# Gated DeltaNet in a hybrid encoder block: decayed keys per chunk in full 128-row tiles, one buffer of U, the queries' norms later

## The chip, the core and the metric

The kernel runs on one core of a Trainium2 chip. The metric is the device time of one execution in microseconds (us). Three runs of the kernel before gave 1604.98, 1605.38 and 1606.62 us; the median is 1605.38 us.

The core's engines are TensorE (PE: matmuls, with its weight loads listed apart as PEld), VectorE (DVE), ScalarE (ACT), GpSimd (POOL) and SyncE (SP), which issues the DMAs here. Each engine works through its own instructions in the order in which they were written into the program, and waits on semaphores for the others.

## The reference

One layer on a sequence of 1024 positions with 1024 channels: an RMS norm, one projection to all branches, a gated DeltaNet (4 heads, key and value width 128), a banded attention (8 heads), two gates, an output projection, and a feed-forward part with a short convolution. The change is in the DeltaNet. It works in chunks of 64 positions; per head a state S (128 x 128) goes from chunk to chunk:

```python
def step(s, xs):
    w_i, uv_i, p_i, qg_i, kd_i, gl_i = xs
    u = uv_i - jnp.einsum('bhid,bhde->bhie', w_i, s)
    o = jnp.einsum('bhid,bhde->bhie', qg_i, s) + jnp.einsum('bhij,bhje->bhie', p_i, u)
    s = gl_i[..., None, None] * s + jnp.einsum('bhid,bhie->bhde', kd_i, u)
    return s, o
```

`w` and `uv` come from a triangular solve in each chunk, `kd` are the keys of the chunk times their decay to its end: `kd_c = k * jnp.exp(G[..., -1:] - G)[..., None]`. The einsum with `kd` sums over the 64 positions of one chunk.

## The kernel before

Two chunks stand together on the 128 partitions as a pair p (8 pairs, `NT`); e is the chunk in the pair and `r` its 64 partitions. The big projections (`proj_half`, lines 118 to 133) are matmuls of 128 x 128 weights with 512 columns into `psph`, three for each product (high and low halves of both operands). For each of the four heads h these steps follow one another:

- `gdn_qkv`: three projections and convolutions (`conv_silu`) give keys `kf`, values `vf` and queries in `WQ`.
- `gdn_prep`: PE transposes the keys into PSUM (`psk`), ACT copies them to `nKs`, writes the decayed keys `Kd` (line 431) and squares them (`jk`, line 433) into the sums `ssk`. From `ssk` POOL computes the norm's factors up to `nks`.
- `gdn_prep2`: PE transposes the values (`psv`), ACT copies them to `Vs`; decay matrices (`psd`, `decb`, `decT`), the products of the keys (`psG`, `psQ`), the matrix `nL`, which goes through DRAM to `Lr`. These, `psW`, `psU` and `psk` all take tiles of one PSUM pool, `psa`, which has three buffers: a fourth tile waits until the first is read.
- `gdn_solve`: 31 pairs of DVE instructions (`tmp`, `Zt`, lines 506 and 508) invert the 32 x 32 blocks; the result goes through DRAM to `zt`.
- `gdn_apply`: PE finishes the inverse (`psB`, `psZ`) and makes W (`psW`) and U (`psU`).
- `gdn_chain`: the 16 steps of the state. Per step PE multiplies with S (`psws`, line 568), DVE updates the 64 rows of U (line 569) and writes O (line 570), PE multiplies `Kd` with U (`pss`, line 572), DVE makes the next S (line 574). After the second chunk of a pair comes `pso` (line 578).
- `gdn_rms`, `gdn_out`, `gdn_qnorm`: norm and output of O; `gdn_qnorm` squares the queries into `sqq`, and PE sums them (`psn`).

The loop over heads (lines 652 to 716) interleaves the chain of head h with the preparation of head h + 1. The tuples C1, C2, C3, OUT, APP, APK and QN say after how many steps each part is placed, and a scheduler with priorities (`tc.high_priority`, `behind()`) then sets the order on each engine; the projections of the coming head and of the gates fill PE in between. At the start `first_rms` (line 224) loads x in blocks of 128 rows (`xt`) into tiles that are free by then, and `wv` (line 268) are the first values' weights.

Of the kernel before, what the change touches and what calls it, by code (L numbers as in the profile page):

```python
# [8 lines left out]
F32 = mybir.dt.float32  # L9
F32R = mybir.dt.float32r  # L10
# [6 lines left out]
P = 128  # L17
D = 1024
# [16 lines left out]
OUT = (0, 3, 5, 3, 8)  # L35
APP = (10, 10, 10, 2)
APK = (7, 4, 3, None)
QN = (7, 3, 4, 5)
PR0 = 1
GFILL = (4, 4, 5, 5, 4)  # L40
PRI = 4000
# [5 lines left out]
def hybrid_kernel(ctx: ExitStack, tc: tile.TileContext, a):  # L47
# [176 lines left out]
    def first_rms(e):  # L224

        s = slice(e * HN, (e + 1) * HN)
        psr = psa.tile([P, HN], F32, tag="a", name="psrb")
        for i in range(4):
            xt = gp.tile([P, D], F32, tag=("Kd", "U")[i % 2], name="xt", bufs=2)
            nc.sync.dma_start(xt, a["x"][(4 * e + i) * P:(4 * e + i + 1) * P, :])  # L230
            ssq = sml.tile([P, 1], F32, tag="ssq", name="ssq")
            nc.scalar.activation(xt, xt, AF.Square, accum_out=ssq)
            ms = sml.tile([P, 1], F32, tag="ms", name="ms")
            nc.vector.tensor_scalar(out=ms, in0=ssq, scalar1=1.0 / D, scalar2=EPS, op0=ALU.mult, op1=ALU.add)
            rs = sml.tile([P, 1], F32, tag="rs", name="rs")
            rsqrt(rs, ms)
            dg = gp.tile([P, P], F32, tag=("Zt", "tmp", "Z11", "B1")[i], name="dg")
            nc.vector.tensor_scalar_mul(dg, ident, rs)
            mm(psr[:, i * P:(i + 1) * P], ones2, dg, start=True, stop=True)
        nc.scalar.copy(rb[:, s], psr)  # L240
# [24 lines left out]
    nea = prm[:, 61:65]  # L265
    nc.scalar.activation(nea, nea, AF.Exp)
    nc.vector.tensor_scalar_mul(nea, nea, -1.0)
    wraw, whi, wlo = (gw.tile([P, KT, P], dt, tag=tg, name="wv") for dt, tg in ((F32, "sq"), (F32R, "nKs"), (F32R, "Vs")))
    nc.sync.dma_start(wraw, a["w_tiles"][2 * GH])
    split(wraw, whi, wlo, nc.vector)  # L270
    ws.append((whi, wlo))
# [82 lines left out]
    for i in range(1):  # L354
        t_ = gp.tile([P, NT, P], F32, name=f"zt{i}")
        nc.gpsimd.memset(t_, 0.0)
        zts.append(t_)

    def bc3(ap, n):

        return ap.unsqueeze(2).broadcast_to([P, NT, n])
# [38 lines left out]
    def gdn_prep(c):  # L400
        h, WQ, kf, vf = c["h"], c["WQ"], c["kf"], c["vf"]
        qv = WQ[:, :, 64:192]

        m64 = [m_.unsqueeze(1).broadcast_to([P, NT, CH]) for m_ in (mgt64, mle64)]
        gms = []
        for m_, n_ in zip(m64, ("gs", "gi")):
            gh = gp.tile([P, NT, CH], F32R, tag="gmh", name=n_ + "h")
            gl = gp.tile([P, NT, CH], F32R, tag="gml", name=n_ + "l")
            en = nc.gpsimd if n_ == "gs" else nc.vector
            en.tensor_tensor(out=gh, in0=m_, in1=bc3(ghi.bitcast(F32)[:, :, h], CH), op=ALU.mult)  # L410
            en.tensor_tensor(out=gl, in0=m_, in1=bc3(glo.bitcast(F32)[:, :, h], CH), op=ALU.mult)
            gms.append((gh.rearrange("p n j -> p (n j)"), gl.rearrange("p n j -> p (n j)")))
        nKs = gw.tile([P, NT, P], F32, tag="nKs", name="nKs")
        Kd = gp.tile([P, NT, P], F32, tag="Kd", name="Kd", bufs=2)
        Vs = gw.tile([P, NT, P], F32, tag="Vs", name="Vs")
        ssk = gp.tile([P, NT], F32, tag="ssk", name="ssk", bufs=2)
        rk = gp.tile([P, NT], F32, tag="rk", name="rk", bufs=2)
        bv = gp.tile([P, NT], F32, tag="bv", name="bv", bufs=2)
        nb = gp.tile([P, NT], F32, tag="nb", name="nb", bufs=2)
        nks = gp.tile([P, NT], F32, tag="nks", name="nks", bufs=2)  # L420
        jk = gp.tile([P, P], F32, tag="jk", name="jk")
        pks = []
        for e in range(2):
            psk = psa.tile([P, HN], F32, tag="a", name="psk")
            for i in range(4):
                p = 4 * e + i
                nc.tensor.transpose(out=psk[:, i * P:(i + 1) * P], in_=kf[:, p * P:(p + 1) * P], identity=ident)
            pks.append(psk.rearrange("p (n d) -> p n d", d=P))
            nc.scalar.copy(nKs[:, 4 * e:4 * e + 4, :], pks[e])
            for i in range(4):  # L430
                nc.scalar.activation(Kd[:, 4 * e + i, :], pks[e][:, i, :], AF.Copy, scale=eg[:, 2, 4 * e + i, h:h + 1])
            for i in range(4):
                nc.scalar.activation(jk, nKs[:, 4 * e + i, :], AF.Square, accum_out=ssk[:, 4 * e + i:4 * e + i + 1])
        nc.vector.tensor_scalar_add(ssk, ssk, EPS)
        rsqrt(rk, ssk)
        nc.gpsimd.tensor_mul(bv, beta[:, :, h], rk)
        nc.gpsimd.tensor_mul(nb, bv, rk)
        nc.gpsimd.tensor_mul(nks, nb, neg0[:, :, h])
        c.update(nKs=nKs, Kd=Kd, Vs=Vs, nks=nks, bv=bv, nb=nb, gms=gms, m64=m64)
# [83 lines left out]
    def gdn_apply(c):  # L523
        nL, zt = c["nL"], zts[0]
        Z11 = gp.tile([P, NT, 32], F32, tag="Z11", name="Z11")
        psx1 = psa.tile([P, HN], F32, tag="a", name="psB1")
        B1 = gp.tile([P, NT, 32], F32, tag="B1", name="B1")
        psx2 = psa.tile([P, HN], F32, tag="a", name="psZ21")
        for e in range(2):
            r0 = slice(e * CH, e * CH + 32)  # L530
            r1 = slice(e * CH + 32, (e + 1) * CH)
            nc.vector.transpose(out=Z11[r0], in_=zt[r0, :, r0])
            for p in range(NT):
                mm(psx1[r0, p * 32:(p + 1) * 32], nL[r1, p, 0:32], zt[r1, p, r1], start=True, stop=True)
            nc.scalar.copy(B1[r0].rearrange("p n j -> p (n j)"), psx1[r0, 0:256])
            for p in range(NT):
                mm(psx2[r0, p * 32:(p + 1) * 32], Z11[r0, p, :], B1[r0, p, :], start=True, stop=True)
            nc.scalar.copy(zt[r0, :, r1], psx2[r0, 0:256].rearrange("p (n j) -> p n j", j=32))

        WQ, nKs, Vs = c["WQ"], c["nKs"], c["Vs"]  # L540
        U = gp.tile([P, NT, P], F32, tag="U", name="U", bufs=2)
        for q in range(2):
            n = slice(4 * q, 4 * q + 4)
            psW = psa.tile([P, HN], F32, tag="a", name="psW")
            for i in range(4):
                mm(psW[:, i * P:(i + 1) * P], nKs[:, 4 * q + i, :], zt[:, 4 * q + i, :], start=True, stop=True)
            w4 = psW.rearrange("p (n e i) -> p n e i", e=2, i=CH)
            for e in range(2):
                nc.scalar.copy(WQ[:, n, e * 192:e * 192 + CH], w4[:, :, e, :])
            psU = psa.tile([P, HN], F32, tag="a", name="psU")  # L550
            for i in range(4):
                mm(psU[:, i * P:(i + 1) * P], zt[:, 4 * q + i, :], Vs[:, 4 * q + i, :], start=True, stop=True)
            nc.scalar.copy(U[:, n, :], psU.rearrange("p (n d) -> p n d", d=P))
        c["U"] = U

    def gdn_chain(c):

        h, WQ, U, Kd, pt = c["h"], c["WQ"], c["U"], c["Kd"], c["pt"]
        O = gp.tile([P, NT, P], F32, tag="O", name="O")
        c["O"] = O  # L560
        S = gp.tile([P, P], F32, tag="S", name="S", bufs=3)
        nc.vector.memset(S, 0.0)
        for p in range(NT):
            for e in range(2):
                r = slice(e * CH, (e + 1) * CH)
                rx = slice((1 - e) * CH, (2 - e) * CH)
                ps = psc.tile([P, P], F32, tag="c", name="psws")
                mm(ps, WQ[:, p, e * P:(e + 1) * P], S, start=True, stop=True)
                nc.vector.tensor_add(U[r, p, :], ps[r], U[r, p, :])
                nc.vector.tensor_scalar_mul(O[rx, p, :], ps[rx], eg[rx, 1, p, h:h + 1])  # L570
                ps2 = psc.tile([P, P], F32, tag="c", name="pss")
                mm(ps2, Kd[r, p, :], U[r, p, :], start=True, stop=True)
                S2 = gp.tile([P, P], F32, tag="S", name="S", bufs=3)
                last["dve"] = nc.vector.scalar_tensor_tensor(out=S2, in0=S, scalar=eg[:, 3 + e, p, h:h + 1], in1=ps2,
                                                             op0=ALU.mult, op1=ALU.add).ins
                S = S2
            ps3 = psc.tile([P, P], F32, tag="c", name="pso")
            mm(ps3, pt[:, p, :], U[:, p, :], start=True, stop=True)
            nc.vector.tensor_add(O[:, p, :], ps3, O[:, p, :])
            yield  # L580
# [13 lines left out]

    def gdn_qnorm(c):

        sqq = gw.tile([P, NT, P], F32, tag="sq", name="sqq")
        nc.scalar.activation(sqq, c["WQ"][:, :, 64:192], AF.Square)
        psn = psc.tile([P, 8], F32, tag="c", name="psn")
        for p in range(NT):  # L600
# [1190 lines left out]
```

## Time and profile before

| What | Value |
|---|---|
| median of three runs | 1605.38 us |
| the profiled execution | 1603.48 us |
| its span in the trace | 1601.4 us |
| PE busy | 1561.8 us, 98% |
| DVE busy | 1123.8 us, 70% |
| ACT busy | 695.8 us, 43% |
| POOL busy | 589.4 us, 37% |

The span runs from the first to the last instruction of the trace; some 2 us of the execution's time lie around it. The DeltaNet's part ends at about 452 us of the span; the attention follows until about 760 us, and then the output projection and the feed-forward part. A row of a timeline shows the start, the time, the engine, the line, the operation and its tiles, and in brackets how long the engine sat idle before and for whom. A float32 matmul of 128 columns is two records (x2).

### The profile page before, as it was taken

What the parts mean: (1) busy time and instruction counts of PE and PEld (TensorE: products, weight loads), DVE (VectorE), ACT (ScalarE), POOL (GpSimd) and SP (SyncE); (2) the same over time, 40 slices, a digit from 0 to 9 for tenths busy, and PEclk for the clock granted to TensorE, in tenths of its full rate; (3) what the DMA queues carried; (4) which work ended last, traced back from release to release, by engine and by line L of the source; (5) the groups of instructions that cost most, each with busy time, mean ns of one, the idle gap of its engine ahead of it and who ended that gap; (6) DMA issues with size and microseconds to landing.
All of it is one profiled execution on the core that took longest, in us unless ns stands there. A gap on an engine that the chain in (4) does not pass through costs nothing.

```text
span 1601.4 us, 21106 instructions
## 1 busy us (share of the span) xinstructions
PE 1561.8 (98%) x7687; PEld 1254.7 (78%) x7687; DVE 1123.8 (70%) x2150; ACT 695.8 (43%) x1376; POOL 589.4 (37%) x445
## 2 busy tenths in 40 slices
PE   8999999999999999999999999999999999999997
PEld 6777776877777777778887887888888888788885
DVE  6795867948436867865665567677777777787787
ACT  7535333352224645554322335444444444333344
POOL 2422212212021101011220248877777776232352
PEclk9999999999999999999999999999999999999998
DMA  7021121122131101111654222233333322775523
GB/s 292 27 81 53 53 73 44 56 61 82 44 122 49 35 23 35 43 53 61 204 171 152 85 93 83 68 111 117 114 114 113 99 99 73 238 247 172 176 92 138
DMA packets 74503, 162.02 MB, mean 101 GB/s; under 512 B 15648, under 2 KB 16928, under 8 KB 74400
## 3 DMA queue, kind: packets, MB, share of 16 engines
q1 hardware_dynamic: 74400, 160.68, 30.2%
q8 instruction: 60, 0.98, 0.3%
q14 instruction: 43, 0.35, 0.1%
HBM read 120.55 MB, written 40.11 MB: 100 GB/s over the span
## 4 chain that ended last, share of the span: by engine, by line
PE 78%; DVE 7%; ACT 2%; issue 1%; DMA 1%; SPq 0%; POOL 0%; POOLq 0%; DVEq 0%; ACTq 0%
PE psph L52 27%; PE psd L52 7%; PE pb L52 7%; PE psout L52 5%; PE pc L52 5%; PE pa L52 4%; PE pb L1131 3%; PE pss L52 3%; PE psd L1483 3%; PE pso L52 3%; PE pc L1131 2%; PE pa L1131 2%; PE psp L852 2%; PE psws L52 1%; DVE tmp L506 1%
## 5 line engine op out<-in xcount | busy, mean ns | idle before, releaser
L82 POOL TENSOR_TENSOR wlo<-wraw,whi 128x1024 fp32r<-128x1024 f32 (+1 forms) x57 | 119.9, 2104 | 481.1 <-ACT whi L81 446.0
L52 PE MATMUL psph<-BH,whi 128*128 128x512 f32 x688 | 281.5, 409 | 9.7 <-ACT BH L220 5.2
L52 PE MATMUL psph<-BL,whi 128*128 128x512 f32 x688 | 278.2, 404 | 0.0
L52 PE MATMUL psph<-BH,wlo 128*128 128x512 f32 x688 | 275.9, 401 | 1.7 <-POOL wlo L82 1.7
L52 PEld LDWEIGHTS psph<-BH,whi 128*128 128x128 f32 x688 | 130.5, 190 | 37.0 <-ACT BH L220 5.9
L1145 POOL TENSOR_TENSOR ol<-wraw,oh 128x512 fp32r<-128x512 f32 x110 | 150.6, 1386 | 9.1 <-ACT oh L1145 9.1
L52 PEld LDWEIGHTS psph<-BH,wlo 128*128 128x128 f32 x688 | 130.5, 190 | 26.5 <-POOL wlo L82 2.1
L52 PEld LDWEIGHTS psph<-BL,whi 128*128 128x128 f32 x688 | 130.3, 189 | 24.5 <-DVE BL L221 1.5
L52 PE MATMUL psd<-wdl,ah 128*128 128x512 f32 (+1 forms) x311 | 121.8, 392 | 5.5 <-DVE wdl L1145 5.5
L1145 POOL TENSOR_TENSOR al<-araw,ah 128x1024 fp32r<-128x1024 f32 (+1 forms) x28 | 68.5, 2447 | 145.3 <-ACT ah L1145 145.2
L1145 POOL TENSOR_TENSOR wraw<-wraw 128x512 f32<-128x512 f32 x86 | 119.4, 1389 | 4.9
L1483 PE MATMUL psd<-wdh,al 128*128 128x512 f32 (+1 forms) x311 | 120.9, 389 | 0.0
L52 PE MATMUL psd<-wdh,ah 128*128 128x512 f32 (+1 forms) x311 | 119.8, 389 | 0.0
L1145 ACT CAST oh<-wraw 128x512 fp32r<-128x512 f32 x110 | 67.6, 619 | 102.0 <-POOL wraw L1145 101.9
L1145 DVE TENSOR_TENSOR wdl<-W,wdh 128x512 fp32r<-128x512 f32 x77 | 88.4, 1186 | 29.4 <-ACT wdh L1145 29.3
L1145 ACT CAST ah<-araw 128x1024 fp32r<-128x1024 f32 (+1 forms) x39 | 40.6, 1040 | 116.7 <-issue 51.9
L81 ACT CAST whi<-wraw 128x1024 fp32r<-128x1024 f32 (+2 forms) x61 | 55.2, 905 | 78.1 <-PE psph L52 54.9
L1145 POOL TENSOR_TENSOR gl<-wraw,gh 128x512 fp32r<-128x512 f32 x42 | 55.8, 1330 | 69.6 <-ACT gh L1145 69.6
L52 PEld LDWEIGHTS psd<-wdl,ah 128*128 128x128 f32 x311 | 58.8, 189 | 20.1 <-DVE wdl L1145 8.1
L1131 PE MATMUL pa<-BH,gh 128*128 128x512 f32 x176 | 68.6, 390 | 0.0
L52 PE MATMUL pa<-BL,gh 128*128 128x512 f32 x176 | 68.5, 389 | 0.0
L52 PE MATMUL pa<-BH,gl 128*128 128x512 f32 x176 | 68.5, 389 | 0.0
(341 smaller groups left out, 3826.1 us busy)
## 6 DMA issues: line engine op xcount, KB each, us to landing
wraw<-w_up SPq DMA_DIRECT2D x44, 512.0 KB, 5.0
wraw<-w_tiles SPq DMA_DIRECT2D x42, 512.0 KB, 3.5
araw<-dA SPq DMA_DIRECT2D x77, 256.0 KB, 3.0
dA<-yu SPq DMA_DIRECT2D x33, 512.0 KB, 3.1
W<-w_down SPq DMA_DIRECT2D x44, 256.0 KB, 4.8
xt<-x SPq DMA_DIRECT2D x16, 512.0 KB, 5.3
dG<-gt SPq DMA_DIRECT2D x16, 512.0 KB, 2.7
ta<-dG SPq DMA_DIRECT2D x16, 256.0 KB, 2.8
```

The source lines that it names most:

```text
L52: last["mm"] = nc.tensor.matmul(*args, **kw).ins
L81: nc.scalar.copy(hi, src)
L82: (eng or nc.gpsimd).tensor_tensor(out=lo, in0=src, in1=hi.bitcast(F32), op=ALU.subtract)
L506: nc.vector.tensor_tensor(out=tmp[:, :, 0:i], in0=Zt[:, :, 0:i], in1=Lr[:, i:i + 1, 0:i].broadcast_to([P, 8, i]), op=ALU.mult)
L852: nc.tensor.transpose(out=psp[:, i * P:(i + 1) * P], in_=Sb[:, (i0 + i) * P:(i0 + i + 1) * P], identity=ident)
L1131: i = nc.tensor.matmul(ps, wh[:, k], xh[:, k], start=start and k == 0, stop=False, **kw)
L1145: return lambda *args, **kw: tc.keep_in_program_order(f(*args, **kw))
L1483: i = nc.tensor.matmul(ps, al[:, j, ts], wh[:, es], start=False, stop=stop, **kw)
```

## The change

There are five edits.

1. `Kd` is now two fixed tiles (`Kds`, for heads in turn) of 128 x 8 x 2 x 128, set to zero once by POOL. For each pair there are two 128 x 128 blocks; block e holds the decayed keys of chunk e on its 64 partitions and zeros on the others. ACT writes each with a copy of 64 partitions, so 16 copies a head where there were 8; the squares stand ahead of these copies in the program.
2. The state's update multiplies all 128 rows, `Kd[:, p, e, :]` with `U[:, p, :]`, where it took the 64 rows `r` of both.
3. U has one buffer instead of two.
4. `sqq` uses the tile of `zs` instead of one of its own, and QN puts the queries' norms two steps later for the second head and three later for the third.
5. At the start the loads `xt` take three tiles in turn (those of U, `Lr` and `vf`) instead of four, and `wv` takes the tile of `kf`.

```diff
-QN = (7, 3, 4, 5)
+QN = (7, 5, 7, 5)
...
         for i in range(4):
-            xt = gp.tile([P, D], F32, tag=("Kd", "U")[i % 2], name="xt", bufs=2)
+            pool, tag = ((gp, "U"), (gp, "Lr"), (gw, "vf"))[i % 3]
+            xt = pool.tile([P, D], F32, tag=tag, name="xt")
             nc.sync.dma_start(xt, a["x"][(4 * e + i) * P:(4 * e + i + 1) * P, :])
...
-    wraw, whi, wlo = (gw.tile([P, KT, P], dt, tag=tg, name="wv") for dt, tg in ((F32, "sq"), (F32R, "nKs"), (F32R, "Vs")))
+    wraw, whi, wlo = (gw.tile([P, KT, P], dt, tag=tg, name="wv") for dt, tg in ((F32, "kf"), (F32R, "nKs"), (F32R, "Vs")))
...
+    Kds = []
+    for i in range(2):
+        t_ = gp.tile([P, NT, 2, P], F32, name=f"Kd{i}")
+        nc.gpsimd.memset(t_, 0.0)
+        Kds.append(t_)
+
...
-        Kd = gp.tile([P, NT, P], F32, tag="Kd", name="Kd", bufs=2)
+        Kd = Kds[h % 2]
...
             for i in range(4):
-                nc.scalar.activation(Kd[:, 4 * e + i, :], pks[e][:, i, :], AF.Copy, scale=eg[:, 2, 4 * e + i, h:h + 1])
+                nc.scalar.activation(jk, nKs[:, 4 * e + i, :], AF.Square, accum_out=ssk[:, 4 * e + i:4 * e + i + 1])
             for i in range(4):
-                nc.scalar.activation(jk, nKs[:, 4 * e + i, :], AF.Square, accum_out=ssk[:, 4 * e + i:4 * e + i + 1])
+                for c_ in range(2):
+                    r = slice(c_ * CH, (c_ + 1) * CH)
+                    nc.scalar.activation(Kd[r, 4 * e + i, c_, :], pks[e][r, i, :], AF.Copy,
+                                         scale=eg[r, 2, 4 * e + i, h:h + 1])
...
-        U = gp.tile([P, NT, P], F32, tag="U", name="U", bufs=2)
+        U = gp.tile([P, NT, P], F32, tag="U", name="U")
...
                 ps2 = psc.tile([P, P], F32, tag="c", name="pss")
-                mm(ps2, Kd[r, p, :], U[r, p, :], start=True, stop=True)
+                mm(ps2, Kd[:, p, e, :], U[:, p, :], start=True, stop=True)
...
-        sqq = gw.tile([P, NT, P], F32, tag="sq", name="sqq")
+        sqq = gp.tile([P, NT, P], F32, tag="zs", name="sqq")
```

The order on the engines changes at three places that matter here. On ACT, the preparation of the second head stands beside the chain of the first. Before, the last squares of the keys stand behind the second copy of U (`L553`), and the scaling of `nKs` follows:

```order
L431 ACTIVATE Kd<-psk,eg 128x128 x2
L433 ACTIVATE jk,ssk<-nKs 128x128
L553 COPY U<-psU 128x512
L433 ACTIVATE jk,ssk<-nKs 128x128 x3
L618 ACTIVATE jk,sqo<-O 128x128
L81 CAST whi<-wraw 128x1024
L618 ACTIVATE jk,sqo<-O 128x128
L487 ACTIVATE nKs<-nKs,nks 128x128 x8
```

Now the same place reads:

```order
L438 ACTIVATE jk,ssk<-nKs 128x128
L442 ACTIVATE Kd_293<-psk,eg 64x128
L628 ACTIVATE jk,sqo<-O 128x128
L442 ACTIVATE Kd_293<-psk,eg 64x128
L628 ACTIVATE jk,sqo<-O 128x128
L442 ACTIVATE Kd_293<-psk,eg 64x128 x2
L563 COPY U<-psU 128x512
L497 ACTIVATE nKs<-nKs,nks 128x128 x6
```

All eight squares stand ahead of the second copy of U now, and four of the sixteen copies of `Kd` behind the last square; `Vs` (not shown) follows behind the scaling of `nKs` in both.

On PE, the preparation of the fourth head stands in the chain of the third. Before, right behind the first pair's `pso`:

```order
L52 MATMUL pss<-U,Kd 128x128
L52 MATMUL pso<-U,ptA_285 128x128
L447 MATMUL psv<-ident,vf 128x128 x8
L52 MATMUL psd<-gsh,mleR 128x512
L52 MATMUL psd<-gsl,mleR 128x512
L52 MATMUL psws<-S,WQ 128x128
L52 MATMUL psph<-BH,wlo 128x512
L52 MATMUL psph<-BH,whi 128x512
L52 MATMUL psd_3264<-gih,mgtR 128x512
```

Now the transposes of the values (`psv`) still stand behind that `pso`, but the decay matrix `psd` is here, in the second pair:

```order
L52 MATMUL pss<-U,Kd_291 128x128
L52 MATMUL psph<-BH,wlo 128x512
L52 MATMUL psph<-BH,whi 128x512
L52 MATMUL psph<-BL,whi 128x512
L52 MATMUL psws<-S,WQ 128x128
L52 MATMUL psph<-BH,wlo 128x512
L52 MATMUL psph<-BH,whi 128x512
L52 MATMUL psph<-BL,whi 128x512
L52 MATMUL psd<-gsh,mleR 128x512
L52 MATMUL psd<-gsl,mleR 128x512
L52 MATMUL pss<-U,Kd_291 128x128
L52 MATMUL pso<-U,ptA_285 128x128
```

Between `psv` and `psd` there are now three matmuls of the state and nine of the projections. In the chains of the first two heads `psd` still follows `psv` at once, behind the third pair; between two matmuls of the state stand mostly three of the projections, as before.

On SP's queue at the start, with what each DMA waits for, before:

```order
L230 DMA xt<-x 128x1024 [waits DMAHW6_49]
L230 DMA xt<-x 128x1024 [waits DMAHW7_49]
L230 DMA xt<-x 128x1024 [waits DMAHW0_49]
L230 DMA xt<-x 128x1024 [waits DMAHW1_49]
L269 DMA wv<-w_tiles 128x1024 [waits DMAHW2_49]
```

and now:

```order
L231 DMA xt<-x 128x1024 [waits DMAHW6_49]
L231 DMA xt<-x 128x1024 [waits DMAHW7_49]
L231 DMA xt<-x 128x1024 [waits DMAHW0_49]
L231 DMA xt<-x 128x1024 [waits DMAHW1_49,Activation_49]
L270 DMA wv<-w_tiles 128x1024 [waits DMAHW2_49]
```

The order is the same, but the fourth load of x waits for ACT, which must have squared the first block, and everything behind it on SP waits too.

## Rows read from the trace of the kernel before

**Rows 1.** Page, part 1: busy us, share of the span, instructions of each engine.

```profile
PE 1561.8 (98%) x7687; PEld 1254.7 (78%) x7687; DVE 1123.8 (70%) x2150; ACT 695.8 (43%) x1376; POOL 589.4 (37%) x445
```

**Rows 2.** Page, part 4: the chain that ended last, shares of the span by engine.

```profile
PE 78%; DVE 7%; ACT 2%; issue 1%; DMA 1%; SPq 0%; POOL 0%; POOLq 0%; DVEq 0%; ACTq 0%
```

**Rows 3.** Timeline of PE in the last chain: start us, us, line, operation, tiles.

```profile
432.95 0.40 PE L52 MATMUL psph<-BL,whi 128*128 128x512 f32 x1
433.19 0.38 PE L52 MATMUL psws<-S,WQ 128*128 128x128 f32 x2
433.32 0.48 PE L52 MATMUL psph<-BH,wlo 128*128 128x512 f32 x1
...
433.88 0.39 PE L52 MATMUL psph<-BL,whi 128*128 128x512 f32 x1
434.19 0.48 PE L52 MATMUL pss<-U,Kd 64*128 64x128 f32 x2
434.61 0.50 PE L52 MATMUL psph<-BH,wlo 128*128 128x512 f32 x1
...
436.10 0.40 PE L52 MATMUL psph<-BL,whi 128*128 128x512 f32 x1
436.43 0.48 PE L52 MATMUL pss<-U,Kd 64*128 64x128 f32 x2
436.84 0.49 PE L52 MATMUL pso<-U,ptA 128*128 128x128 f32 x2
437.09 0.48 PE L52 MATMUL psph<-BH,wlo 128*128 128x512 f32 x1
```

**Rows 4.** Timeline of DVE, same stretch: idle time before and its releaser in brackets.

```profile
433.61 0.28 DVE L569 TENSOR_TENSOR U<-psws,U 64x128 f32<-64x128 f32 x1 [0.40 <-PE psws L52]
...
434.72 0.35 DVE L574 SCALAR_TENSOR_TENSOR S<-S,eg,pss 128x128 f32<-128x128 f32 x1 [0.44 <-PE pss L52]
```

**Rows 5.** Waits in 134 to 452 us: in total, times, longest.

```profile
DVE U L569 <- PE psws L52: 40.4, 40, 9.4
...
DVE S L574 <- PE pss L52: 16.0, 37, 0.8
```

**Rows 6.** Busy us by window: length, PE, PEld, DVE, ACT, POOL, then clock, DMA.

```profile
128.90:226.10 97.20, 93.96 (x563) 73.90 (x563) 72.97 (x175) 40.00 (x106) 24.66 (x24) 1.00 0.19 59
...
405.50:452.00 46.50, 45.59 (x281) 33.94 (x281) 23.53 (x63) 11.92 (x32) 4.77 (x2) 1.00 0.12 42
```

**Rows 7.** Timeline of ACT, preparation of the third head.

```profile
236.16 1.15 ACT L431 ACTIVATE Kd<-psk,eg 128x128 f32<-128x128 f32 x4
...
241.51 0.31 ACT L433 ACTIVATE jk<-nKs 128x128 f32<-128x128 f32 x1
...
245.26 2.45 ACT L487 ACTIVATE nKs<-nKs,nks 128x128 f32<-128x128 f32 x8 [2.07 <-POOL nks L438]
...
247.91 1.04 ACT L448 COPY Vs<-psv 128x512 f32<-128x512 f32 x2
```

**Rows 8.** Timelines of DVE and PE where the third head's solve ends.

```profile
225.20 0.43 DVE L532 STREAM_TRANSPOSE Z<-zt 32x256 f32<-32x256 f32 x1 [2.94 <-DMA zt<-dZ]
...
226.15 0.69 PE L52 MATMUL psB<-zt,nL 32*32 32x32 f32 x16
```

**Rows 9.** Timelines of SP, ACT, PE and POOL at the start.

```profile
11.15 0.33 SPq L269 DMA_DIRECT2D wv<-w_tiles  x1
...
14.88 1.06 ACT L232 ACTIVATE xt<-xt 128x1024 f32<-128x1024 f32 x1 [0.42 <-DMA xt<-x]
...
20.00 1.05 ACT L81 CAST wv<-wv 128x1024 fp32r<-128x1024 f32 x1
...
24.50 0.39 PE L52 MATMUL psph<-BH,wv 128*128 128x512 f32 x1
...
2.51 0.95 POOL L356 MEMSET zt<- 128x1024 f32 x1
...
16.30 0.56 POOL L78 TENSOR_TENSOR rs<-ms,mhalf 128x1 f32<-128x1 f32 x1 [12.71 <-DVE ms L234]
```

## The prediction, made before the changed kernel had run

> **What bounds the kernel now.** I read the page's busy times first, then the chain that ended last, then the timelines of PE and DVE in the chain of the state, then what waits there. PE is busy 98% of the span [rows 1] and makes 78% of the chain that ended last, DVE 7% and ACT 2% [rows 2]. So a microsecond taken from PE's own work is a microsecond of the whole, unless PE then arrives somewhere too early and waits. The change touches only the DeltaNet. The span from one head's `psB` to the next is 97.2 us, of which PE is busy 93.96 and DVE 72.97 [rows 6].
>
> **The drains that go.** The reader should set the steps in the last chain side by side [rows 3]. A projection matmul of 512 columns takes about 0.24 us from its start to the next start. `psws`, 128 rows of float32, fits in: from the projection ahead of it (432.95) to the one behind it (433.32) are 0.37 us. `pss` has the same columns but 64 rows, and there the same distance is 433.88 to 434.61, 0.73 us. PE marks no wait: U was ready at 433.89 (433.61 + 0.28 [rows 4]), 0.30 ahead of `pss`. So PE stands still ahead of the 64-row matmul and behind it, 0.36 us in all, where nothing but the row count differs from `psws`. With `pso` behind it the stretch is 436.10 to 437.09, 0.99 us; with `pss` priced as `psws` and `pso` at the 0.13 us that `psws` itself takes (433.19 to 433.32) it would be 0.50, so 0.49 go.
>
> There are 4 heads, 8 pairs and 2 chunks: 64 steps, half of them followed by `pso`. 32 x 0.36 + 32 x 0.49 = 11.5 + 15.7 = 27.2 us of PE's time, 6.8 per chain. That a 128-row `pss` costs what `psws` does is the assumption; the two then differ in nothing that a row shows.
>
> The Trainium skill, "TensorEngine Tiling (Array Packing)", section Key Properties, says that a change of the array's tiling mode drains TensorE, and 64 rows are a mode of their own there; the 0.36 us of [rows 3] agree, and by that rule the sum stays at 27.2. The same page's Overview speaks against the change: a contraction of 64 or less should be run as row tiles, for up to twice the speed, and by it full rows with zeros could gain nothing. No row shows two of these matmuls side by side, since chunk 1 needs the S that chunk 0 left; I go by the rows.
>
> **Does the chain keep up?** With the drains gone PE reaches the next matmul of the state sooner, and the data must be there. From `psws` to U is 0.42 us (433.19 to 433.61), U takes 0.28 [rows 3, 4]: 0.70, while three projections and the matmul itself will fill about 0.9. From `pss` to S is 0.53 and S takes 0.35 [rows 3, 4]: 0.88 at most, 0.77 if S, too, starts 0.42 behind a full-row matmul, against 0.8 to 0.9 of fill. So at most some 0.07 us wait in 32 steps, 2.2 us; I take 0.5, because the shorter latency is that of the row of the same shape. DVE has room for it: it waited 40.4 us for `psws` and 16.0 us for `pss` in these chains [rows 5].
>
> **ACT's preparation.** Per head there are 8 more copies to `Kd`. Four take 1.15 us [rows 7], so 0.29 each and 2.3 us a head; that a copy of 64 partitions costs what one of 128 does is an estimate from that row, since the free size is the same. Nothing of ACT's work goes. Ahead of the last square now stand 12 copies instead of 8, but the second copy of U has moved behind it: 4 x 0.29 less about 0.6, so +0.5 us. From that square (241.51) POOL needs until 245.26 to let ACT scale `nKs`, and `Vs` follows at 247.91 [rows 7]. This path doesn't get shorter, while PE arrives 6 steps earlier in the first two chains (2.6 us) and somewhat less in the third, where `psd` has moved two steps behind `psv`. PE then waits for `Vs` to free its PSUM buffer. Bounds per head: 0, if the scheduler's fill covers it, and 2.6 + 2.3 = 4.9 us, if all shows. I take 1.2, nearer to the row's order, where ACT was about a microsecond behind PE. Three heads: 3.6 us.
>
> **The solve.** DVE reaches the end of the solve, waits 2.94 us for `zt` from DRAM (225.20), and PE starts `psB` at 226.15 [rows 8]: PE comes less than a microsecond after its data. So what PE gains beyond what DVE gains is waited for at `psB`. DVE gains, too, since part of its 24 us of idle time in the loop (97.2 - 72.97 [rows 6]) is the wait for `psws` and `pss`. Bounds per head: 0, and 10 steps, 4.3 us, if DVE gains nothing behind `psG`. I take 0.8, near the small end, as the wait of DVE for PE ([rows 5], 56.4 us in 64 steps, 0.9 a step) is twice what a step loses. Three heads: 2.4 us. In the fourth chain there is no solve: DVE is busy 23.53 of 46.5 us and PE 45.59 [rows 6], so all 6.8 us should show.
>
> **The start.** The fourth `xt` waits for the first square, 14.88 + 1.06 = 15.94, and behind it on SP stand `wv` and the second half of xT. `wv` is issued some 5 us later than at 11.15. Before, it had landed by 20.00 at the latest, 8.85 us after its issue in a full queue; at that rate it lands at 25, and with a cast of 1.05 and about as much for the low half PE would wait 3 us at its 24.50 [rows 9]. With the queue emptied in between it lands near 20 to 21 and nothing waits. Bounds 0 and 3; I take 0, because the queue's other loads were what took the time. The zeroing of `Kds` is four times the 0.95 us of the `zt` memset and lies in POOL's 12.71 us of idle time [rows 9]. In the first head, without a chain beside it, ACT's 2.3 us could show; the decays are ordered earlier there, so I take 0.
>
> **Nothing** for the one buffer of U (written when the last chain has been read to its end), for `sqq` in the tile of `zs` and for the later QN (the same eight small matmuls a head, placed behind `gdn_out`). If that cover fails, it is a wait of PE's side matmuls for one ACT square, about a microsecond a head.
>
> **Sum.** 27.2 - 0.5 - 3.6 - 2.4 = 20.7 us. Profiled execution 1603.48 - 20.7 = 1582.8; the median of the runs is 1.9 above that execution, so 1584.7; I say 1585.
>
> **Rivals.**
> - All of the drains reach the end: ACT and DVE keep up. For it: the chain that ended last has 78% PE [rows 2]. Against: PE is less than a microsecond behind `zt` now [rows 8]. 1605.4 - 27.2 = 1578.
> - The solve takes it back: DVE's path to `zt` doesn't shorten, and PE waits at `psB` for what the first three chains gained. For it: [rows 8]; against: DVE's waits for PE [rows 5]. Only the last chain's 6.8 us are left: 1598 to 1599.
> - Slower: ACT's preparation sets the pace of all heads. `Kd`'s 2.3 us stand ahead of `Vs`, so `nL`, the solve and `psB` come 2.3 us later in each of four heads, 9.2 us, and the first three chains' gain is waited for; the last chain's 6.8 remain. 1605.4 + 2.4 = 1608; with the wait for `wv` at the start fully paid it would be 1611. It decides from the point where `Vs` comes later than now by more than DVE's spare time in the chain. Against: 4 of the 8 added copies stand behind the last square.
> - The change doesn't do what it says: the 0.36 us come not from the rows but from something else about `pss` (that it reads what DVE has just written), and stay. Then 1605 to 1612, by ACT. Against: `psws` reads S, just written by DVE, and pays nothing.
>
> **Chances.** The sum above 0.54, all drains 0.22, the solve 0.12, the slower one 0.06, no effect 0.06. A difference of 0.2% (3.2 us) is about what a measurement of this kernel can tell from none. Faster takes the first three, 0.88; of the last two I give 0.07 to no change and 0.05 to slower. The range reaches from a little below all drains, 1576, to the solve's 1598.
>
> **What would show it.** In the new profile `pss` should be 128 x 128 with a time near the 0.38 us of `psws` for its two records, no longer 0.48 [rows 3], and the stretch from the projection ahead to the one behind it 0.37 us. In the last chain a `pss` should follow the one before it after about 1.9 us instead of 2.24 (434.19 to 436.43 [rows 3]). PE should show waits of 1 to 2 us a head for `Vs` on ACT, and `psB` waits for `zt` below a microsecond. The forecast is wrong if `pss` keeps its gap, if PE waits over 3 us a head at `psB` or before `psd`, or if PE's first matmul of `wv` comes after 26 us.

## The result, and the profile after

The changed kernel took 1597.3 us (median of 4 runs, 1595.4 to 1598.2), the kernel before beside it 1606.0 us: a ratio of 0.995, 95% interval 0.9932 to 0.9968, or 8.7 us less. The forecast was 1585, about 20 us less. The direction was right, the size less than half, and the time lies near the upper end of the range. Two executions in the later runs, one of the kernel before (3091 us) and one of e4 (5489 us), took far longer than all others and stand in no median here.

The page of the changed kernel, parts 1 and 4, answers to [rows 1, 2].

```profile
PE 1549.7 (97%) x7687; PEld 1252.1 (78%) x7687; DVE 1118.0 (70%) x2150; ACT 712.9 (45%) x1408; POOL 596.6 (37%) x447
...
PE 76%; DVE 12%; ACT 6%; DMA 3%; issue 2%; POOL 1%; SPq 1%; POOLq 0%; DVEq 0%; ACTq 0%
```

PE is busy 12.1 us less, but the span is only 5.1 us shorter in the profiled pair (the change's profile is of the longest of its four runs). In the chain that ended last DVE has risen from 7 to 12% and ACT from 2 to 6%: a larger part of that chain is now waiting for other engines.

The drains themselves are gone. The timeline of PE in the last chain, which answers to [rows 3]:

```profile
435.57 0.40 PE L52 MATMUL psph<-BH,whi 128*128 128x512 f32 x1
435.80 0.38 PE L52 MATMUL pss<-U,Kd 128*128 128x128 f32 x2
435.94 0.48 PE L52 MATMUL psph<-BL,whi 128*128 128x512 f32 x1
...
437.80 0.40 PE L52 MATMUL psph<-BL,whi 128*128 128x512 f32 x1
438.03 0.38 PE L52 MATMUL pss<-U,Kd 128*128 128x128 f32 x2
438.25 0.39 PE L52 MATMUL pso<-U,ptA 128*128 128x128 f32 x2
438.39 0.47 PE L52 MATMUL psph<-BH,wlo 128*128 128x512 f32 x1
```

From the projection ahead to the one behind are 0.37 us, where it was 0.73; with `pso` 0.59, where it was 0.99. So a step lost 0.36 or 0.40 us, and 64 steps 32 x 0.36 + 32 x 0.40 = 24.3 us. `pss` in front of `pso` takes 0.22 to the next start and not the 0.13 that I had assumed, so the second term was 2.9 us too large.

What was given back shows in the waits of PE between 120 and 455 us (in total, times, longest). Before:

```profile
PE pss L52 <- DVE U L569: 4.5, 5, 1.8
PE psph L52 <- DVE gt L171: 2.0, 1, 2.0
PE psws L52 <- DVE S L574: 1.4, 1, 1.4
PE psd L52 <- DVE gih L410: 0.7, 1, 0.7
```

After:

```profile
PE psws L52 <- DVE S L584: 5.4, 6, 1.7
PE pss L52 <- DVE U L579: 2.1, 2, 1.2
PE psd L52 <- ACT Kd L442: 2.0, 1, 2.0
PE psB L52 <- DMA zt<-dZ: 1.9, 2, 1.1
PE psd L52 <- DVE gil L418: 1.9, 1, 1.9
PE psph L52 <- DVE u L381: 1.7, 1, 1.7
PE psd L52 <- ACT Vs L458: 1.6, 2, 0.9
```

Together 8.6 us have become 17.0 (with two waits of 0.2 not shown). Three mechanisms stand behind them.

The first is ACT's squares. Timelines of ACT, DVE and PE in the first chain of the changed kernel:

```profile
149.99 0.36 ACT L442 ACTIVATE Kd<-psk,eg 64x128 f32<-64x128 f32 x1
150.38 0.31 ACT L438 ACTIVATE jk<-nKs 128x128 f32<-128x128 f32 x1
...
150.82 0.17 DVE L444 TENSOR_SCALAR ssk<-ssk 128x8 f32<-128x8 f32 x1 [1.74 <-ACT jk L438]
151.02 0.69 DVE L599 TENSOR_TENSOR zs<-psph,rb 128x512 f32<-128x512 f32 x1
151.63 0.34 DVE L584 SCALAR_TENSOR_TENSOR S<-S,eg,pss 128x128 f32<-128x128 f32 x1
...
152.02 0.49 PE L52 MATMUL psws<-S,WQ 128*128 128x128 f32 x2 [1.57 <-DVE S L584]
```

The copies of `Kd` alternate with the squares on ACT. The little sum `ssk` stands on DVE ahead of the update of S, and waits 1.74 us for the last square; S waits behind it, and PE for S. Before, `ssk` started without a wait in all three preparations. The same happens in the next chain (PE waits 1.24 us at 244.20).

The second is POOL. Timelines of POOL, DVE and PE in the second chain:

```profile
250.51 2.52 POOL L82 TENSOR_TENSOR wlo<-wraw,whi 128x1024 fp32r<-128x1024 f32 x1 [3.03 <-ACT whi L81]
...
250.12 0.69 DVE L417 TENSOR_TENSOR gih<-cn,ghi 128x512 fp32r<-128x512 f32 x1
250.73 2.84 DVE L418 TENSOR_TENSOR gil<-cn,glo 128x512 fp32r<-128x512 f32 x1
...
253.62 0.49 PE L52 MATMUL psd<-gil,mgtR 128*128 128x512 f32 x1 [1.87 <-DVE gil L418]
```

`gih` and `gil` are the same operation; the one that runs beside POOL's subtraction `wlo` takes 2.84 us instead of 0.69, and what stands behind it on DVE comes about 2 us late.

The third is PE's clock. Windows of the loop from the first `psB` to the second, which answers to [rows 6], and of 2 us at its start (busy us of the engines, then the granted clock as a share of 2.4 GHz):

```profile
130.20:226.76 96.56, 93.55 (x563) 75.14 (x563) 71.53 (x176) 44.54 (x115) 24.97 (x24) 0.96 0.19 60
...
130.00:132.00 2.00, 1.80 (x28) 1.36 (x29) 1.13 (x2) 0.82 (x2) 0.00 (x0) 1.00 0.98 302
132.00:134.00 2.00, 2.00 (x32) 1.33 (x28) 0.69 (x1) 0.90 (x3) 0.00 (x0) 0.74 0.59 219
134.00:136.00 2.00, 2.00 (x19) 1.71 (x19) 0.00 (x0) 0.36 (x1) 0.00 (x0) 0.50 0.08 27
136.00:138.00 2.00, 2.00 (x9) 1.81 (x9) 0.00 (x0) 0.00 (x0) 0.00 (x0) 0.50 0.00 0
138.00:140.00 2.00, 2.00 (x12) 2.00 (x11) 0.00 (x0) 0.65 (x2) 0.00 (x0) 0.55 0.00 0
140.00:142.00 2.00, 2.00 (x19) 1.93 (x18) 0.99 (x3) 1.24 (x3) 0.00 (x0) 1.00 0.00 0
```

`psB` at 130.20 had waited 1.08 us for `zt`; from about 133 to 139.8 the clock stood at 1.2 GHz, and 3.4 us were lost; that loop took 96.56 us where it had taken 97.20. With two shorter stretches (303 to 308 and 344 to 348 us) the changed kernel lost 6.8 us to the low clock in the DeltaNet, the kernel before 1.7.

What is left can be read at the four `psB`. They started at 128.99, 226.15, 325.79 and 405.52 us before, and at 130.20, 226.76, 325.27 and 405.76 us now: the three loops together became 1.0 us shorter, at the fourth `psB` the changed kernel was still 0.24 us later, and the profiled pair owes its gain in the DeltaNet to the last chain.

### The profile page after: what moved, and what is told of

It is laid out like the page before. It is cut to its first block, busy times and chain, and to the rows that moved or that the text cites. A ratio compares the mean times of both kernels' runs of the same rounds, so it can differ in the third digit from the quotient of the medians.

```text
span 1596.3 us, 21134 instructions
## 1 busy us (share of the span) xinstructions
PE 1549.7 (97%) x7687; PEld 1252.1 (78%) x7687; DVE 1118.0 (70%) x2150; ACT 712.9 (45%) x1408; POOL 596.6 (37%) x447
## 4 chain that ended last, share of the span: by engine, by line
PE 76%; DVE 12%; ACT 6%; DMA 3%; issue 2%; POOL 1%; SPq 1%; POOLq 0%; DVEq 0%; ACTq 0%
PE psph L52 25%; PE psd L52 7%; PE pb L52 7%; PE psout L52 5%; PE pc L52 5%; PE pa L52 4%; PE pb L1141 4%; PE psd L1493 3%; PE pss L52 3%; PE pc L1141 2%; PE pso L52 2%; PE pa L1141 2%; DVE tmp L516 2%; PE psp L862 2%; DVE acc L387 1%
```

## The experiments

All times are medians, and ratios are against the kernel before, run beside them (1605.1 to 1605.3 us; 1606.0 for the change).

| Kernel | us | ratio, 95% interval |
|---|---|---|
| the change | 1597.3 | 0.9950 (0.9932 to 0.9968) |
| e1: the change, `pss` on 64 rows | 1607.5 | 1.0012 (1.0002 to 1.0021) |
| e2: the change, one dense `Kd`, 8 copies | 1593.1 | 0.9925 (0.9914 to 0.9937) |
| e3: the change, copies behind `decT` | 1593.3 | 0.9923 (0.9907 to 0.9939) |
| e4: before, `zt` of the first head later | 1614.4 | 1.0048 (1.0035 to 1.0062) |
| e5: e3, `pss` on 64 rows | 1603.1 | 0.9994 (0.9980 to 1.0008) |
| e6: e3, `wlo` on DVE | 1581.9 | 0.9853 (0.9838 to 0.9868) |
| e7: before, `wlo` on DVE | 1595.6 | 0.9942 (0.9930 to 0.9955) |
| e8: e3, `wlo` on DVE from the second head | 1576.1 | 0.9819 (0.9806 to 0.9832) |
| e9: e8, `pss` on 64 rows | 1592.9 | 0.9927 (0.9912 to 0.9942) |
| e10: the change, `wlo` on DVE from the second head | 1588.9 | 0.9889 (0.9873 to 0.9905) |

**e1: the rows alone.**

```diff
-                mm(ps2, Kd[:, p, e, :], U[:, p, :], start=True, stop=True)
+                mm(ps2, Kd[r, p, e, :], U[r, p, :], start=True, stop=True)
```

> The changed kernel with one line undone: the state's update takes the 64 rows of the chunk again (Kd[r, p, e, :] and U[r, p, :]); zeros, copies, buffers and the order of the rest stay. Theory A (the drains went as priced, and what is missing of the gain was lost elsewhere): pss stands 0.73 us between its neighbours again, about 24 us of PE's time come back, of which up to 10 are covered by waits and by stretches at the low clock that the changed kernel has: 1608 to 1618 us, slower than the kernel before, because ACT's eight more copies a head remain without the gain that pays for them. Theory B (full rows themselves gained little): 1597 to 1601.

Measured 1607.5. The drains are back (timeline of PE in its last chain: 0.74 us from projection to projection):

```profile
436.56 0.40 PE L52 MATMUL psph<-BL,whi 128*128 128x512 f32 x1
436.88 0.48 PE L52 MATMUL pss<-U,Kd 64*128 64x128 f32 x2
437.30 0.50 PE L52 MATMUL psph<-BH,wlo 128*128 128x512 f32 x1
```

So the full rows are worth 10.2 us of their 24.3, and the other edits cost 2.2 (by the interval of the ratio 0.3 to 3.4). Theory B falls; the time is just under theory A's range.

**e2: half of ACT's copies.**

```diff
-                for c_ in range(2):
-                    r = slice(c_ * CH, (c_ + 1) * CH)
-                    nc.scalar.activation(Kd[r, 4 * e + i, c_, :], pks[e][r, i, :], AF.Copy, ...)
+                nc.scalar.activation(Kd[:, 4 * e + i, 0, :], pks[e][:, i, :], AF.Copy, ...)
...
-                mm(ps2, Kd[:, p, e, :], U[:, p, :], start=True, stop=True)
+                mm(ps2, Kd[:, p, 0, :], U[:, p, :], start=True, stop=True)
```

> The changed kernel with 8 copies of 128 rows a head into one dense block of Kd instead of 16 copies of 64 rows into two; both chunks of a pair then multiply the same block. Left out: the separation of the chunks by zeros. Theory A (ACT's extra copies stand ahead of its last square, DVE waits for that square with the update of S queued behind it, and PE waits for S): the waits of PE for S behind ssk (1.57 and 1.24 us) and for Kd (1.99) go, nL comes 3 to 4 us earlier in each head, and the low clock at 132 to 140 us goes with the wait at psB: 1584 to 1590. Theory C (with the drains gone it is DVE's own work in the chain that PE waits for, not ACT's): 1594 to 1598.

The kernel leaves out the zeros that keep the two chunks apart, so it shows a cost and is no candidate. Measured 1593.1: 4.2 us less than the change, between both theories. The waits for `Kd`, behind `ssk` and at `psB` went, but PE waited 6.1 us for U instead of 2.1. Half the copies gone gives 4 us, not the rest.

**e3: the copies later.** They read `nKs`, and stand behind `decT` on ACT.

```diff
-                for c_ in range(2):
-                    ...  # copies from psk, among the squares
...
+        Kd = c["Kd"]
+        for p in range(NT):
+            for c_ in range(2):
+                r = slice(c_ * CH, (c_ + 1) * CH)
+                with behind("decT"):
+                    nc.scalar.activation(Kd[r, p, c_, :], nKs[r, p, :], AF.Copy, scale=eg[r, 2, p, h:h + 1])
```

> The changed kernel, all of the computation, with the 16 copies of Kd placed behind the exponential of decT on ACT and reading the keys from nKs in SBUF instead of psk in PSUM. Theory A: as without the extra copies, since the squares, Vs and the decays no longer stand behind them: 1584 to 1590, no wait for Kd, ssk early, PE's clock full at 130 to 140 us. Theory C: 1594 to 1598. In between, 1590 to 1594, if six microseconds of copies in one piece behind decT hold up a cast of weights or the scaling of Vs that something waits for.

Measured 1593.3, the same 4 us as e2, and inside the range between the two theories. No wait for `Kd`, `Vs` or behind `ssk` is left, but PE waits 5.7 us for S and 4.5 for U. The longest waits now have POOL behind them; two others for S (0.73 and 1.03 us) have `zs` ahead, which waits for ACT's `zth`. Timelines of POOL, DVE and PE:

```profile
146.08 2.37 POOL L82 TENSOR_TENSOR wlo<-wraw,whi 128x1024 fp32r<-128x1024 f32 x1
...
146.46 2.54 DVE L602 SCALAR_TENSOR_TENSOR zs<-zth,zs 128x512 f32<-128x512 f32 x1 [0.44 <-ACT zth L601]
149.03 0.29 DVE L580 TENSOR_TENSOR U<-psws,U 64x128 f32<-64x128 f32 x1
...
149.38 0.49 PE L52 MATMUL pss<-U,Kd 128*128 128x128 f32 x2 [1.65 <-DVE U L580]
```

**e4: what a wait at `psB` costs.** In the kernel before:

```diff
+        if c["h"] == 0:
+            for _ in range(4):
+                nc.vector.tensor_scalar_mul(Zt, Zt, 1.0)
```

> The kernel before, with four DVE instructions more in the first head only (Zt times 1.0, in place, 128 x 256), so that zt comes about 1.2 us later and PE waits for it ahead of psB, as it does in the changed kernel. Theory A (that wait is what lets PE's clock fall in the changed kernel, and the fall costs more than the wait): PE at 1.2 GHz for some 7 us behind psB, 1.2 + 3.4 = 4.6 us more: 1609 to 1611. Theory D (the clock falls there for another reason): only the wait, 1606 to 1608.

Measured 1614.4, 9.1 us more (7.7 by the ratio). My size of the delay was wrong: one of the four ran beside a `wlo` and took 2.53 us, the four 3.51 us. The wait and the clock behind it (PE's row, and the window in which the clock is full again):

```profile
133.50 1.05 PE L52 MATMUL psB<-zt,nL 32*32 32x32 f32 x16 [3.54 <-DMA zt<-dZ]
...
142.00:144.00 2.00, 2.00 (x15) 2.00 (x15) 0.00 (x0) 0.58 (x2) 0.00 (x0) 0.76 0.00 0
```

From 132.7 us, during the wait, to about 143.0 the clock stood at 1.2 GHz. Behind `psB` PE lost 4.7 us by it, and 3.5 + 4.7 is 8.2. So a wait at this place costs more than its length. The profiled execution lost another 3.4 us to the low clock at 382 to 389 us, where the kernel before lost none, so this sum is near the measured difference, but it isn't shown to be all of it. It is not the length alone that decides: `psB` waited 0.89 us in e1 and in e8 without a fall, 0.92 in e10 with one of 3.4 us.

**e5: full rows with ACT out of the way.** e3 with the edit of e1.

> The kernel with the copies of Kd behind decT, with the state's update on the 64 rows of the chunk again. With the run of the late copies it gives what full rows are worth when ACT is out of the way; with the copies in their place they were worth 10 us (1607.2 less 1597.1). Theory V (what ACT's copies held back was the gain of the full rows): full rows are worth 18 to 24 us here, so 1611 to 1617. Theory W (the rest of the gain is lost in the chains to DVE and to the clock, with or without ACT's copies): worth 10 to 14 us, so 1603 to 1607.

Measured 1603.1: full rows are worth 9.8 us here (11.4 by the ratios). Theory V falls: with POOL's subtraction in place, ACT's copies cost 4 us with either number of rows, and taking them out of the way doesn't bring the full rows through.

**e6, e7: POOL's subtraction on DVE.**

```diff
-        split(raw, hi, lo, eng)
+        if eng == "halves":
+            nc.scalar.copy(hi, raw)
+            for k in range(0, nk, nk // 2):
+                ks = slice(k, k + nk // 2)
+                nc.vector.tensor_tensor(out=lo[:, ks], in0=raw[:, ks], in1=hi.bitcast(F32)[:, ks], op=ALU.subtract)
+        else:
+            split(raw, hi, lo, eng)
...  # the DeltaNet's loads of weights ask for "halves"
```

> The kernel with the late copies, in which the low halves of the projections' weights in the DeltaNet (wlo, 128 x 1024) are subtracted on DVE, in two instructions of 128 x 512, instead of on POOL in one of 2.4 us. Theory P (a DVE instruction that reads two operands from SBUF while POOL subtracts is held for as long as POOL takes, and PE, early without the drains, waits for the U or S behind it: 1.65, 1.08, 0.84, 0.86, 1.68 and 1.20 us in the run of the late copies): these waits shrink to a few tenths, 1584 to 1588. Rival: DVE pays 1.4 us for each wlo itself and the chain waits for that instead, 1591 to 1595.

> The kernel before, with the same move of wlo from POOL to DVE and nothing else. Theory P: the waits of PE for U and S behind a held DVE instruction (1.76, 0.66, 0.63, 1.36, 0.91 and 0.52 us) go, 1598 to 1602. Rival (with the drains PE is late enough that they cost nothing, or DVE's own 1.4 us take their place): 1604 to 1607.

Measured 1581.9 and 1595.6: 11.4 and 9.6 us less than without the move, both below theory P's ranges: more than the waits that I had summed in either. In e7 no wait of PE for U or S is left in the chains. In e6 the first `psB` comes late, at 135.10 us, behind waits for `u` and `wlo` of 2.74 and 3.86 us.

**e8, e9: the same from the second head on, with full and with 64 rows.**

```diff
...  # last["h"] is the head whose chain runs, -1 while the first is prepared
-        split(raw, hi, lo, eng)
+        if eng == "halves" and last["h"] >= 0:
+            ...  # two subtractions on DVE
+        else:
+            split(raw, hi, lo, None if eng == "halves" else eng)
```

> The kernel with late copies and wlo on DVE, but POOL keeps wlo while the first head is prepared, where no chain of the state runs and DVE has no idle time (with all of wlo on DVE the first psB came at 135.1 us instead of 128.9, behind waits for u and wlo of 2.7 and 3.9 us). Theory P: the first psB comes at 129 to 130 us again and the rest stays, 1575 to 1579. Rival (what the start gives back is lost at the next psB, to which zt has to come): 1580 to 1583.

> The same kernel with the state's update on the 64 rows of the chunk again: what full rows are worth when neither ACT's copies nor POOL's subtractions hold up the chain. Theory P (the rest of their 24 us was lost to DVE instructions held by POOL): worth 16 to 22 us, so 1593 to 1599. Theory W (they are worth 10 to 12 in any surroundings, the rest goes to latencies of the chain and to the clock): 1587 to 1590.

Measured 1576.1 and 1592.9: e8 beats the kernel before by 29.0 us and the change by 21.2. Full rows are worth 16.8 us here (17.3 by the ratios), inside what theory P said, and theory W falls. In e8, timeline of DVE at the same place as in e3: `wlo` is 0.72 us here, and `zs` has its 0.67.

```profile
145.37 0.72 DVE L94 TENSOR_TENSOR wlo<-wraw,whi 128x512 fp32r<-128x512 f32 x1
146.12 0.29 DVE L586 TENSOR_TENSOR U<-psws,U 64x128 f32<-64x128 f32 x1
146.45 0.34 DVE L587 TENSOR_SCALAR O<-psws,eg 64x128 f32<-64x128 f32 x1
146.72 0.67 DVE L608 SCALAR_TENSOR_TENSOR zs<-zth,zs 128x512 f32<-128x512 f32 x1
```

And the waits of PE in e8, 120 to 455 us (two of 0.4 and 0.3 us, for the attention behind, not shown):

```profile
PE psoT L651 <- ACT O L643: 2.7, 2, 1.6
PE psws L52 <- DVE S L591: 2.1, 3, 1.2
PE pss L52 <- DVE U L586: 1.3, 1, 1.3
PE psB L52 <- DMA zt<-dZ: 0.9, 1, 0.9
```

An earlier `wlo` is not where the gain of e8 comes from: PE waits for no `wlo` between 120 and 455 us in e3. What changes is DVE. Between 120 and 452 us it makes 98 `tmp` of the solve in 39.7 us in e3 and 97 in 28.4 in e8, where no `wlo` on POOL stands beside them, and pays 24.4 us for the 36 halves of `wlo`.

**e10: the change itself with POOL out of the way.** The edit of e8, with the copies where the change has them.

> The changed kernel itself, with wlo on DVE from the second head on and ACT's copies where the change has them. Theory P: the waits for gil, u, U and S behind a held DVE instruction go (1.87, 1.69, 0.86, 1.68, 1.20 us) and the stretch of low clock behind u, those behind ACT's squares and copies stay (1.57, 1.24, 1.99): 1585 to 1589. Rival: 1593 to 1597.

Measured 1588.9, 8.4 us less than the change, at the upper edge of what theory P said. The waits behind `ssk` (1.56 and 1.22 us) and the fall of the clock behind `psB` are still there.

Set side by side, the two hold-ups mask each other. From the change, the later copies alone give 4.0 us (e3), `wlo` on DVE alone 8.4 (e10), both together 21.2 (e8): 8.8 more than the two apart, 6.9 by the ratios, whose four intervals leave about 5 either way. So ACT's copies cost 4.0 us beside POOL's subtraction and 12.8 without it (e10 less e8). And with `wlo` on DVE in both kernels the change as it stands is worth 6.7 us (e7 less e10, where e7 moves the first head's `wlo`, too), no more than with it on POOL: only with the copies out of the way do most of the drains come through. The change with 64 rows and `wlo` on DVE was not run.

## Why the prediction was right in direction and wrong in size

- **The drains** were read rightly: `psph` to `psph` fell to the 0.37 us named. Their sum was 24.3 and not 27.2 us, from the `pso` term. The rule of the Trainium skill ("TensorEngine Tiling (Array Packing)", Key Properties) that a change of mode drains TensorE agrees: the 0.73 us came back with the 64 rows in e1; no run here tried row tiles.
- **"Does the chain keep up?" is the step that failed.** It took 0.5 us, 2.2 at most, from undisturbed latencies (0.70 and 0.77 us). In the change full rows gave 10.2 of 24.3 us, so 14.1 were lost to everything that PE now meets too early. The chain's own share shows where ACT's copies hold up nothing: full rows gave 9.8 us there, and PE waited 10.2 us for U and S with them (e3), 4.8 without (e5). DVE's queue is in order: what makes U or S late is the instruction ahead of it, held by POOL for 2 us or waiting for ACT. POOL's subtraction cost 10.2 us with 64 rows (e5 less e9) and 17.2 with full rows (e3 less e8), so PE's drains had hidden some 7 us of it (6 by the ratios; the four intervals together leave about 5 either way). With it moved, 16.8 of 24.3 us come through (e8 against e9); of the 7.5 left, 4.6 are in e8's named waits, 7.0 us, beyond the 2.4 of e9, which has none but `psoT`.
- The 56.4 us of DVE's waiting that I took for room [rows 5] were misread, too: three of those waits, 5.0, 7.6 and 9.4 us long, stand ahead of the first U of a chain. That leaves 34.3 us, 0.54 a step and not 0.9.
- For the change against e1 the traces name 7.9 us more of waits: 4.6 for U and S, 2.1 for `Kd` and `Vs`, 1.0 at `psB`, 0.2 for O. Each of the 8 added waits costs about 0.16 more than its row says, since a projection's record lasts 0.39 us and the next starts after 0.23: 1.3 us. With 1.7 of clock that is 10.9, so 13.4 us should have been left where 10.2 were measured. Some 3 us stay open.
- **ACT's preparation**, 3.6 us, came out near 4.2 and 4.0 us (e2, e3), in part by luck. It was to be a wait for `Vs` alone; PE waits 1.6 us for `Vs`, 2.0 for `Kd` and 2.8 behind `ssk`, which I did not see, and the 4 us hold only beside POOL's subtraction. The copies cost more than the 0.29 us taken: ACT is busy 17.1 us longer, not 9.2.
- **The solve**, 2.4 us: `psB` waited 0.80 us in the fourth head, nothing in the second and third, and 1.08 in the first, where I had taken 0. The rival "the solve takes it back" gave 1598 to 1599, near the measured time, and as it says, little but the last chain's gain is left; but it came about another way: at the second and third `psB` PE comes after `zt`.
- **The start**: PE's first matmul of `wv` came at 25.83 us, within what I had allowed, and the first `psdec` 1.15 us earlier than before (61.61 instead of 62.76); by `psB` this had become 1.2 us later. e1 costs 2.2 us and ACT's copies 4.0 to 4.4, so the edits at the start, of U and of QN together cost nothing that shows; that they gave some 2 us is not clear of noise (e5 against the kernel before: 0.9980 to 1.0008).
- **The clock** was not in the sum at all. Its mean over the runs was 0.9932 for the change and 0.9949 for the kernel before (16 runs beside e1 to e4): 10.9 and 8.2 us at a loss of 1 - clock, so by this estimate 2.7 us of the missing 12; in the profiled pair's DeltaNet it was 5.1.
- In the last chain `pss` follows `pss` after 1.85 us in the steps that wait for nothing, as forecast (1.9), and the 15 steps from its first `pss` to its last fell from 35.5 to 30.8 us. That chain, which has no solve and no preparation beside it, gave 4.7 of the 6.8 us. From first to last `pss` the first three chains took 43.9, 45.4 and 42.7 us before, 40.4, 42.4 and 43.0 in the change: the third gained nothing, and what the first two gained was mostly lost outside these stretches, since their loops became only 0.6 and 1.1 us shorter. In e8 the four took 38.3, 38.6, 38.3 and 29.6 us.

## What to carry to other kernels

When an engine that bounds the kernel is relieved, price each wait that it will meet by the instruction that stands *ahead* of its producer in that producer's queue, and not by the producer's own latency. Look first for work on an engine off the critical path that makes another engine's instruction longer: here moving a 2.4 us subtraction off POOL was worth 9.6 us alone, about as much as the change itself. And try the relief once with all such neighbours moved, since one can hide behind another: the same full rows were worth 10 us with POOL's subtraction in place, and 17 with it and ACT's copies out of the way.

## What the runs showed of the hardware that I had not expected

- A DVE instruction that takes two operands from SBUF and comes up beside POOL's `wlo` (2.4 us) stands until `wlo` ends and up to some half a microsecond longer: `zs` took 2.54 us instead of 0.67, `gil` 2.84 instead of 0.69. A `Zt` times 1.0, with one operand, took 2.53 instead of 0.29. The Trainium skill says in "GPSIMD Engine Reference", Key points, that POOL shares its SBUF interfaces with VectorE, with contention for instructions that read two operands from SBUF or run in a two-port mode. The trace agrees for two operands; in which mode `Zt` ran, no row shows.
- The chain's own U, O and S, each with an operand in PSUM, are not held themselves; they come late when a held instruction stands ahead. Timelines of POOL and DVE in the changed kernel:

```profile
162.23 2.59 POOL L82 TENSOR_TENSOR wlo<-wraw,whi 128x1024 fp32r<-128x1024 f32 x1 [0.50 <-ACT whi L81]
...
162.60 0.29 DVE L579 TENSOR_TENSOR U<-psws,U 64x128 f32<-64x128 f32 x1
162.93 0.34 DVE L580 TENSOR_SCALAR O<-psws,eg 64x128 f32<-64x128 f32 x1
163.47 0.35 DVE L584 SCALAR_TENSOR_TENSOR S<-S,eg,pss 128x128 f32<-128x128 f32 x1 [0.21 <-PE pss L52]
```

- Copies on ACT of 64 partitions, in turn on the two halves, follow each other after 0.38 us (7 in 2.62), those of 128 partitions after 0.25 (4 in 1.15 [rows 7]): the small ones take 0.36 us each and don't overlap, the large ones 0.39 and do, so 16 copies of half the partitions cost more than twice what 8 of all do. Whether the change of halves is the reason was not tried.
- Runs of one kernel with a lower mean clock tend to be longer: the kernel before took 1603.4 us at a mean of 0.997 and 1608.7 at 0.991. The clock is not all of it, since 1604.8 us came at 0.993 and at 0.998.
